# Six branch gates of a hybrid decoder layer computed by seven half-size products, spread between the branch products

## The chip, the cores and the metric

The kernel runs on one core of a Trainium2 chip. The metric is the device time of one execution in microseconds (us); lower is better. Engines are named as in the profile: PE is the matrix engine (TensorE), PEld its weight loads, DVE is VectorE, ACT is ScalarE, POOL is GpSimd, and SP issues most of the DMA transfers.

## The reference, cut to what matters

One decoder layer over 512 tokens of width 1024: a gated feed-forward half step, a mixer (dilated attention beside an mLSTM), and a second half step. The change is in the mixer's last part, the merge:

```python
A = dilated sliding-window attention        # att: (512, 512)
M = mLSTM matrix memory                     # ml:  (512, 1024)
merged = sigmoid(g_A) * (att @ W_A) + sigmoid(g_M) * (ml @ W_M)
x = x + RMSNorm_post(merged @ W_out)
# g_A, g_M: 1024 columns each of the input projection h @ W_in, h = RMSNorm_pre(x), (512, 1024)
```

Everything is float32.

## The kernel before

**How products are made.** PE multiplies in a reduced format (fp32r), so each operand is split into a high part (an ACT cast) and a low part (a DVE subtraction), and each product is three: high by high, high by low, low by high. The normalised activations lie transposed, 128 columns of the width by 512 tokens per block, as `hTh` and `hTl` (eight such blocks each). `load_w` loads a weight tile of 128 x 1024 (512 KB) into one of three `wf` buffers, casts it into one of five `wh` buffers (line 86) and subtracts into one of five `wl` buffers (line 88). `ws` (line 178) then issues, for a width of 8 blocks, 24 matmuls of 512 columns.

**Feed-forward parts.** Both already use a scheme of seven half-size products (Strassen's, in Winograd's form): a 2 x 2 block product is made from seven products of half size instead of eight, with sums of weight blocks and of activation blocks made first, and sums of the results afterwards. There a class `Order` (line 249) fixes the order on DVE, ACT and SP by hand.

**The merge.** The merged width has eight blocks, `dt` = 0 to 7. For each, `branch_gates(dt)` makes both gates, `wgm[dt, 0]` and `wgm[dt, 1]`, by two calls of `ws` (48 matmuls of 512 columns, row `p<-hTh_mx,wh_gm` in the profile), and ACT takes tanh of both into `t1` (line 1104). Gates 0 and 1 are made while the last mLSTM head is finished. The loop over `dt` then makes the two branch products, attention in 12 matmuls (`p2[0]`) and mLSTM in 24 (`p2[1]`), multiplies them with the gates (DVE, line 1150), adds (line 1151), splits the sum into `meTh` (ACT, line 1152) and `meTl` (DVE, line 1153), and ends with `branch_gates(dt + 2)`. After the loop, `down` multiplies by W_out in 192 matmuls (`acc_o`), and the results pass through the post norm into `xs`, the four tiles that hold x through the whole kernel.

**What sets the order.** Each engine runs its own instructions in one fixed order and waits at an instruction for what that needs. Outside the `Order` class that order is not the text's: a scheduler in the language's tile layer lays all instructions out with its own notion of their durations, and buffers (`bufs=5`) come free when their last reader is done.

Of the kernel before, what the change touches and what calls it, by code (L numbers as in the profile page):

```python
# [32 lines left out]
WMAX = 1024  # L33
# [6 lines left out]
def tile_hybrid_block(ctx: ExitStack, tc: tile.TileContext, a: dict):  # L40
    nc = tc.nc

    ids = ctx.enter_context(tc.tile_pool(name="ids", bufs=1))
    wpool = ctx.enter_context(tc.tile_pool(name="wpool", bufs=1))
    hpool = ctx.enter_context(tc.tile_pool(name="hpool", bufs=1))
    const = ctx.enter_context(tc.tile_pool(name="const", bufs=1, side="right"))
    act = ctx.enter_context(tc.tile_pool(name="act", bufs=1, side="right"))
# [10 lines left out]
    work = Work()  # L58
# [20 lines left out]
    def load_w(src, name, n=1024, after=()):  # L79
        wf = act.tile([P, WMAX], F32, tag="wf", bufs=3, name=f"wf_{name}")[:, :n]  # L80
        nc.sync.dma_start(wf, src)
        with ExitStack() as st:
            for i in after:
                st.enter_context(tc.issue_after(i))
            wh = wpool.tile([P, WMAX], F32R, tag="wh", bufs=5, name=f"wh_{name}")[:, :n]
            nc.scalar.copy(wh, wf)  # L86
            wl = wpool.tile([P, WMAX], F32R, tag="wl", bufs=5, name=f"wl_{name}")[:, :n]
            nc.vector.tensor_tensor(wl, wf, wh.bitcast(F32), op=ALU.subtract)  # L88
        return wh, wl

    def gain(src, name, eng=None):
        g = work.tile([P, D], F32, tag="gain", bufs=2, name=f"g_{name}")
        (eng or nc.gpsimd).dma_start(g, src.partition_broadcast(P))
        return g
# [16 lines left out]
        nc.vector.scalar_tensor_tensor(v, ss[:, 0:1], (4 if half else 1) * EPS, ss[:, 1:2], op0=ALU.add, op1=ALU.add)  # L111
        return rsqrt(v, 1, name)

    xs = [const.tile([P, D], F32, name=f"x{t}") for t in range(NT)]

    dram = ctx.enter_context(tc.tile_pool(name="dram", bufs=1, space=bass.MemoryType.DRAM))

    def scratch(name, *where):
# [55 lines left out]
    def ws(out, w, nk, xh, xl, tok=slice(0, T)):  # L174
        wh, wl = w
        terms = [(wh, x, k) for k in range(nk) for x in (xh, xl)] + [(wl, xh, k) for k in range(nk)]
        for n, (wt, x, k) in enumerate(terms):
            nc.tensor.matmul(out, lhsT=wt[:, k * P:(k + 1) * P], rhs=x[:, k, tok], start=n == 0,  # L178
                             stop=n == len(terms) - 1)
# [45 lines left out]
    def step(out, xh, xl, wh, wl, t, b, first, last):  # L225
        tk = slice(t * P, (t + 1) * P)
        cs = slice(b * 512, (b + 1) * 512)
        for n, (x, w) in enumerate(((xh, wh), (xl, wh), (xh, wl))):
            nc.tensor.matmul(out, lhsT=x[:, tk], rhs=w[:, cs], start=first and n == 0, stop=last and n == 2,  # L229
                             skip_group_check=True)  # L230
# [178 lines left out]
    class Down:  # L409
# [8 lines left out]
        def tt(self, out, p, q, op):  # L418
            self.do("vector", "tensor_tensor", out, p, q, op=op)
# [74 lines left out]
        def product(self, s):  # L494
            k, g = s[0], int(s[1])
            (xh, xl), (wh, wl) = self.x.pop(s), self.w.pop(s)
            if k in "pq":
                for b in range(2):
                    for i in range(2):
                        step(self.accs[i + 2 * (k == "q")][b], xh[:, i * P:], xl[:, i * P:], wh, wl, 0, b, False, False)  # L500
                return
            for n, (x, w) in enumerate(((xh, wh), (xh, wl), (xl, wh))):
                for m in range(2):
                    for i, o in enumerate(self.out[k]):
                        tk, cs = slice(m * H + i * P, m * H + (i + 1) * P), slice(m * T, (m + 1) * T)
                        nc.tensor.matmul(o, lhsT=x[:, tk], rhs=w[:, cs], start=k in "1256" and g + m + n == 0,
                                         stop=False, skip_group_check=True)
# [132 lines left out]
    with new_pool("ffn_a") as fa:  # L640
# [11 lines left out]
        for t in range(2):  # L652
            h = prenorm_first(t, g_pre, (hbuf + tbuf)[t])
# [6 lines left out]
        for t in range(2, NT):  # L660
            h = prenorm_first(t, g_pre, (hbuf + tbuf)[t], turned)
# [20 lines left out]
    hTh, hTl = hT  # L682
# [188 lines left out]
    def m_qk_proj(h, pi, between=None):  # L871
        pq = pair(f"pm{h}{pi}")
        w = [load_w(a["wmqk"][h, 2 * pi + b], f"mqk{h}{pi}{b}") for b in range(2)]
        ws(pq[0], w[0], KD, hTh, hTl)
        if between is not None:
            between()
        ws(pq[1], w[1], KD, hTh, hTl)
        return pq
# [15 lines left out]
        nc.vector.tensor_tensor(lo, zz, hi.bitcast(F32), op=ALU.subtract)  # L894


    pq0 = [pair(f"pq0{g}") for g in range(2)]
    w0 = [[load_w(a["wqk"][0, g, b], f"qk0{g}{b}", after=pins if g + b else ()) for b in range(2)] for g in range(2)]
    by_halves([(pq0[g], w0[g]) for g in range(2)], hTh, hTl, todo)
    for g in range(2):  # L900
        qk_of[0, g] = qk_evac(0, g, pq0[g])
    qk_proj(0, 2)
    for half in range(2):
        v0_proj(half)
    v12 = v12_proj(0)
# [188 lines left out]

    t1s = {}

    def branch_gates(dt):
# [4 lines left out]
        t1 = work.tile([P, 2, T], F32, tag=("h", "tmp")[dt % 2], bufs=1, name=f"t1_{dt}")  # L1102
        for b in range(2):
            nc.scalar.activation(t1[:, b, :], p1[b], AF.Tanh, scale=0.5)
        t1s[dt] = t1

    E = m_decay(0)
    for h in range(MH):
        vm, so = m_vo(h)
        EE = m_scores(h, qk, E)  # L1110
        if h + 1 < MH:
            qk = new_mqk(h + 1)
            m_qk_conv(h + 1, 0, m_qk_proj(h + 1, 0), qk)
        else:
            branch_gates(0)
        m_out(h, EE, vm, so)
        if h + 1 < MH:
            m_qk_conv(h + 1, 1, m_qk_proj(h + 1, 1), qk)
            E = m_decay(h + 1)
        else:  # L1120
            branch_gates(1)
        m_turn(h, so)
    lctx.close()

# [2 lines left out]
    mg = gctx.enter_context(tc.tile_pool(name="merge", bufs=1))  # L1127
# [8 lines left out]
            return mlT[k // 2][self.i][:, k % 2, tok]  # L1136

    mlTh, mlTl = Tiles(0), Tiles(1)
    wA = None
    for dt in range(KD):  # L1140
        if dt % 2 == 0:
            wA = load_w(a["wA"][dt // 2], f"wA{dt}")
        wM = load_w(a["wM"][dt], f"wM{dt}")
        p2 = pair(f"p2_{dt}")
        o = (dt % 2) * 512
        ws(p2[0], (wA[0][:, o:o + 512], wA[1][:, o:o + 512]), HEADS, atth, attl)
        ws(p2[1], wM, KD, mlTh, mlTl)
        t1 = t1s[dt]
        for b in range(2):
            nc.vector.scalar_tensor_tensor(t1[:, b, :], t1[:, b, :], 1.0, p2[b], op0=ALU.add, op1=ALU.mult)  # L1150
        nc.vector.tensor_tensor(t1[:, 0, :], t1[:, 0, :], t1[:, 1, :], op=ALU.add)
        nc.scalar.mul(meTh[:, dt, :], t1[:, 0, :], 0.5)
        nc.vector.scalar_tensor_tensor(meTl[:, dt, :], t1[:, 0, :], 0.5, meTh[:, dt, :].bitcast(F32),
                                       op0=ALU.mult, op1=ALU.subtract)
        if dt + 2 < KD:
            branch_gates(dt + 2)

    g_mpost = gain(a["mix_post_g"], "mpost")
    g_f2pre = gain(a["ffn2_pre_g"], "f2pre")
    hT2 = []  # L1160
# [117 lines left out]
```

## Time and profile before

| | |
|---|---|
| median of 3 runs | 1358.43 us (1358.39 to 1358.49) |
| profiled execution | 1358.6 us, span of its instructions 1356.8 us |
| PE busy | 1342.3 us of the span |
| DVE / ACT busy | 967.8 / 601.7 us |
| merge loop, first branch product to first W_out product | about 131 us, from 831.4 to 961.9 us |
| W_out product and post norm after it | from 961.9 us on |
| granted PE clock, mean | 0.998 |

A row of a group reads: source line, engine, operation, output <- inputs, shape, count | busy us in all, mean ns of one | idle time of that engine just before, and what ended it. A row of the timeline begins with start and length in us.

### The profile page before, as it was taken

To read this page: it belongs to the slowest core of one execution; us is meant where nothing else is said; L and a number is where in the kernel's file an instruction comes from. 1 tells how busy PE (TensorE), PEld (TensorE's weight loads), DVE (VectorE), ACT (ScalarE), POOL (GpSimd) and SP (SyncE) were. 2 spreads that over 40 slices of the span, in tenths; PEclk is the share of its full clock that TensorE was granted. 3 is DMA by queue.
4 is the path that set the end of the run, shared out by engine and by line. 5 is a ranking of instruction groups with operands and counts; after the bars stand their busy time and mean duration, and the time that the engine had idled before them with its cause. 6 is when DMAs were issued, how large, how long until landed. Compare 5 with 4: busy or idle time off the path is not lost.

```text
span 1356.8 us, 19908 instructions
## 1 busy us (share of the span) xinstructions
PE 1342.3 (99%) x7976; PEld 1192.8 (88%) x7976; DVE 967.8 (71%) x1482; ACT 601.7 (44%) x969; POOL 32.8 (2%) x56
## 2 busy tenths in 40 slices
PE   8999999999999999999999999999999999999998
PEld 8899999878898888888888888888889999998786
DVE  7799898996772885775756754334378798997983
ACT  5444444554633532445535443222264444444552
POOL 1000000000200000000000000000010000000000
PEclk9999999999999999999999999999999999999999
DMA  5233333654233422422222232233213333335541
GB/s 202 93 109 103 106 104 109 232 174 152 66 95 118 140 82 89 144 74 78 78 78 78 79 117 73 102 97 109 93 46 111 94 97 107 108 106 196 173 148 62
DMA packets 41661, 150.11 MB, mean 111 GB/s; under 512 B 4716, under 2 KB 4716, under 8 KB 41312
## 3 DMA queue, kind: packets, MB, share of 16 engines
q1 hardware_dynamic: 39600, 141.08, 31.7%
q0 software_dynamic: 1968, 7.76, 1.8%
q8 instruction: 62, 1.02, 0.3%
q14 instruction: 31, 0.25, 0.1%
HBM read 144.63 MB, written 4.19 MB: 110 GB/s over the span
## 4 chain that ended last, share of the span: by engine, by line
PE 89%; DVE 6%; ACT 2%; issue 2%; DMA 1%; SPq 0%; DVEq 0%; POOLq 0%; ACTq 0%
PE p L178 11%; PE qb_b L321 9%; PE qb_a L321 9%; PE pq L178 8%; PE pm L178 6%; PE qa_a L321 4%; PE qa_b L321 4%; PE acc_o L229 3%; PE pvo L997 2%; PE pvo L999 2%; PE pvo L998 2%; PE pg_a L188 2%; PE pg_b L188 2%; PE pq L188 2%; PE pg_b L178 2%; PE pg_a L178 2%
## 5 line engine op out<-in xcount | busy, mean ns | idle before, releaser
L178 PE MATMUL pq<-hTh_mx,wh_qk 128*128 128x512 f32 x160 | 63.2, 395 | 0.0
L178 PE MATMUL pq<-hTl_mx,wh_qk 128*128 128x512 f32 x160 | 62.4, 390 | 0.0
L88 DVE TENSOR_TENSOR wl_qk<-wf_qk,wh_qk 128x1024 fp32r<-128x1024 f32 x24 | 29.3, 1220 | 40.2 <-ACT wh_qk L86 29.9
L178 PE MATMUL pm<-hTh_mx,wh_mqk 128*128 128x512 f32 x128 | 50.3, 393 | 0.0
L997 PE MATMUL pvo<-wh_vo,hTh_mx 128*128 128x512 f32 x128 | 50.2, 392 | 0.0
L178 PE MATMUL pm<-hTl_mx,wh_mqk 128*128 128x512 f32 x128 | 49.9, 390 | 0.0
L178 PE MATMUL p<-hTh_mx,wh_gm 128*128 128x512 f32 x128 | 49.9, 390 | 0.0
L999 PE MATMUL pvo<-wl_vo,hTh_mx 128*128 128x512 f32 x128 | 49.8, 389 | 0.0
L178 PE MATMUL p<-hTl_mx,wh_gm 128*128 128x512 f32 x128 | 49.8, 389 | 0.0
L998 PE MATMUL pvo<-wh_vo,hTl_mx 128*128 128x512 f32 x128 | 49.8, 389 | 0.0
L86 ACT CAST wh_qk<-wf_qk 128x1024 fp32r<-128x1024 f32 x24 | 25.0, 1045 | 54.1 <-PE pw L741 27.3
L1150 DVE SCALAR_TENSOR_TENSOR t<-t,p 128x512 f32<-128x512 f32 x16 | 11.0, 688 | 42.7 <-PE p L178 42.7
L88 DVE TENSOR_TENSOR wl_mqk<-wf_mqk,wh_mqk 128x1024 fp32r<-128x1024 f32 x16 | 19.6, 1222 | 29.7 <-ACT wh_mqk L86 25.3
L178 PE MATMUL pq<-hTh_mx,wl_qk 128*128 128x512 f32 x160 | 39.6, 389 | 0.0
L888 DVE SCALAR_TENSOR_TENSOR z<-pm,cw,z 128x511 f32<-128x511 f32 (+2 forms) x48 | 35.2, 742 | 1.4 <-ACT z L886 0.9
L249 ACT CAST wh_a<-cd_a 128x1024 fp32r<-128x1024 f32 x18 | 18.9, 1049 | 39.0 <-DVE cd_a L249 39.0
L321 PE MATMUL qa_a<-hTl_f,wh_a 128*128 128x256 f32 x144 | 36.1, 283 | 0.0
L321 PE MATMUL qa_b<-hTl_f,wh_b 128*128 128x256 f32 x144 | 36.1, 283 | 0.0
L321 PE MATMUL qa_a<-hTh_f,wh_a 128*128 128x256 f32 x144 | 36.1, 283 | 0.0
L321 PE MATMUL qa_b<-hTh_f,wh_b 128*128 128x256 f32 x144 | 36.1, 283 | 0.0
L249 ACT CAST wh_b<-cd_b 128x1024 fp32r<-128x1024 f32 x18 | 18.9, 1049 | 37.9 <-DVE cd_b L249 37.9
L178 PEld LDWEIGHTS pq<-hTh_mx,wl_qk 128*128 128x128 f32 x160 | 30.0, 188 | 6.2
(679 smaller groups left out, 4396.3 us busy)
## 6 DMA issues: line engine op xcount, KB each, us to landing
wf_qk<-in_wqk SPq DMA_DIRECT2D x24, 512.0 KB, 3.6
B_a<-in_wdq SPq DMA_DIRECT2D x21, 512.0 KB, 3.8
B_b<-in_wdq SPq DMA_DIRECT2D x21, 512.0 KB, 4.4
g_a<-in_wgu SPq DMA_DIRECT2D x18, 512.0 KB, 3.7
u_a<-in_wgu SPq DMA_DIRECT2D x18, 512.0 KB, 3.8
g_b<-in_wgu SPq DMA_DIRECT2D x18, 512.0 KB, 3.8
u_b<-in_wgu SPq DMA_DIRECT2D x18, 512.0 KB, 3.8
wf_mqk<-in_wmqk SPq DMA_DIRECT2D x16, 512.0 KB, 3.3
```

The source lines that it names most:

```text
L86: nc.scalar.copy(wh, wf)
L88: nc.vector.tensor_tensor(wl, wf, wh.bitcast(F32), op=ALU.subtract)
L178: nc.tensor.matmul(out, lhsT=wt[:, k * P:(k + 1) * P], rhs=x[:, k, tok], start=n == 0, stop=n == len(terms) - 1)
L188: nc.tensor.matmul(outs[b][:, tok], lhsT=ws_[b][w][:, k * P:(k + 1) * P], rhs=x[:, k, tok], start=i + k + hf == 0, stop=hf == 1 and i == 2 ...
L229: nc.tensor.matmul(out, lhsT=x[:, tk], rhs=w[:, cs], start=first and n == 0, stop=last and n == 2, skip_group_check=True)
L249: self.last[eng] = getattr(getattr(nc, eng), fn)(*args, **kw).ins
L321: nc.tensor.matmul(out, lhsT=wt[:, i * P:(i + 1) * P], rhs=y[:, i, :], start=first and n == 0, stop=last and n == len(terms) - 1, skip_gro ...
L888: nc.vector.scalar_tensor_tensor(z[:, s:], src[:, :T - s], cw[:, ct, 3 - s:4 - s], z[:, s:], op0=ALU.mult, op1=ALU.add)
L997: nc.tensor.matmul(out, lhsT=hTh[:, k, tk], rhs=wh[:, cs], start=k == 0, stop=False)
L998: nc.tensor.matmul(out, lhsT=hTl[:, k, tk], rhs=wh[:, cs], start=False, stop=False)
L999: nc.tensor.matmul(out, lhsT=hTh[:, k, tk], rhs=wl[:, cs], start=False, stop=k == KD - 1)
L1150: nc.vector.scalar_tensor_tensor(t1[:, b, :], t1[:, b, :], 1.0, p2[b], op0=ALU.add, op1=ALU.mult)
```

## The change

Gates 2 to 7 are made by seven products of half size. Gates 0 and 1 stay as they were.

- `make_parts` builds, beside the end of mLSTM head 3, the sums of activation blocks: four full blocks (`full`), four differences, and their splits `part5`, `part7`, `part4`; the block that `hTh`/`hTl` hold in one corner is overwritten by part 6 once gate 1 is made. Parts 5 and 7 lie in the tiles of x, part 4 in the tiles of the gains.
- To free those, x is stored to DRAM (`xkeep`) before the mixer and loaded back into `xs` after the merge loop, by POOL's DMA queue; the gains `g_mpost` and `g_f2pre` are loaded after it, once part 4 has been read.
- `unit` makes one gate pair: it loads both weight tiles as `g` and `u`, makes four sums of half tiles (DVE), casts and subtracts 3.5 tiles' worth of weights in four takes (`(1,2)`, `(4)`, `(7,5)`, `(6,3)`), and issues 7 x 12 matmuls of 256 columns into two PSUM banks, `qa` (products 1, 2) and `qb` (6, 7 and 4 in one half, 5 and 3 in the other). Product 2 is added in the bank to product 1, after ACT has copied product 1 out (`q1`). DVE adds the rest in four steps.
- `unit` is a generator with three stops, and the loop takes it up between the branch products: products 1, 6, 5 after `p2[0]`, products 2, 7, 3 after `p2[1]`, product 4 after the next block's `p2[0]`.

```diff
+    def unit(n, srcs, r, q1, first_out):
+        g, u = (act.tile([P, 2, Q], F32, tag="wf", bufs=3, name=f"{'gu'[b]}_{n}") for b in range(2))
+        for t, src in zip((g, u), srcs):
+            nc.sync.dma_start(t, src.rearrange("p (q c) -> p q c", c=Q))
...
+        take((1, 2), g)
+        take((4,), u[:, 1:2, :])
+        tt(u[:, 1, :], u[:, 0, :], u[:, 1, :], ADD)
+        tt(u[:, 0, :], g[:, 0, :], u[:, 0, :], SUB)
+        tt(g[:, 0, :], u[:, 1, :], g[:, 0, :], SUB)
+        tt(g[:, 1, :], g[:, 1, :], g[:, 0, :], SUB)
+        take((7, 5), u)
+        take((6, 3), g)
+        pa, pb = bank(f"qa_{n}"), bank(f"qb_{n}")
+        qa, qb, qc = pa[:, 0:H], pb[:, 0:H], pb[:, H:T]
...
+        product(qa, 1, True, False)
+        nc.scalar.copy(q1, qa)
+        product(qb, 6, True, False)
+        product(qc, 5, False, False)
+        tt(r[:, :, H:T], pb.rearrange("p (a b) -> p a b", b=H), q1[:, None, :].broadcast_to([P, 2, H]), ADD)
+        yield
+        product(qa, 2, False, True)
+        first_out(r[:, 0, 0:H], qa)
+        product(qb, 7, False, False)
+        tt(r[:, 1, H:T], qb, r[:, 1, H:T], ADD)
+        product(qc, 3, False, True)
+        tt(r[:, 0, H:T], qc, r[:, 0, H:T], ADD)
+        yield
+        product(qb, 4, False, True)
+        tt(r[:, 1, 0:H], qb, q1, ADD)
+        yield
...
+    for t in range(NT):
+        nc.gpsimd.dma_start(xkeep[t], xs[t])
...
         ws(p2[0], (wA[0][:, o:o + 512], wA[1][:, o:o + 512]), HEADS, atth, attl)
+        for _ in late_gates:
+            pass
+        next(gates_, None)
         ws(p2[1], wM, KD, mlTh, mlTl)
+        next(gates_, None)
...
-        if dt + 2 < KD:
-            branch_gates(dt + 2)
-
+        late_gates = gates_
+
+    xs[:] = new_xs()
+    for t in range(NT):
+        nc.gpsimd.dma_start(xs[t], xkeep[t])
```

The order that the scheduler makes of it is shown at three places of block `dt` = 4. First PE. Before, the block's 36 branch matmuls (`p2_4_0`, `p2_4_1`) and then the 48 of gate 6 (`p1_6`) follow each other, each group on a PSUM bank of its own:

```order
L178 MATMUL p2_4_0_8316<-atth_3891,wl_wA4_8308 128x512 x4
L178 MATMUL p2_4_1_8317<-mlm0h0_6539,wh_wM4_8312 128x512
...
L178 MATMUL p2_4_1_8317<-mlEh3_7816,wl_wM4_8314 128x512 x2
L178 MATMUL p1_6_0_8371<-hTh_mx_3745,wh_gm60_8361 128x512
...
L178 MATMUL p1_6_1_8372<-hTh_mx_3745,wl_gm61_8369 128x512 x8
L178 MATMUL p2_5_0_8430<-atth_3891,wh_wA4_8306 128x512
```

Now, behind `p2_4_0` stand products 7, 3 and 4 of gate 5 (`wh7`, `wh6`, `wh4`; a tile holds two products' weights and has the first one's number), product 1 of gate 6 around product 4, then product 2 of gate 6 (`wh1` again) and product 6 (`wh6`):

```order
L180 MATMUL p2_4_0_8550<-atth_3891,wl_wA4_8542 128x512 x4
L959 MATMUL qb_gm5_8431<-part7h_7632,wh7_gm5_8422 128x256
...
L959 MATMUL qb_gm5_8431<-hTh_mx_3745,wh6_gm5_8426 128x256
...
L959 MATMUL qa_gm6_8604<-hTh_mx_3745,wh1_gm6_8584 128x256
L959 MATMUL qb_gm5_8431<-part4h_7638,wh4_gm5_8414 128x256
...
L959 MATMUL qa_gm6_8604<-hTh_mx_3745,wl1_gm6_8585 128x256 x4
L959 MATMUL qa_gm6_8604<-hTh_mx_3745,wh1_gm6_8584 128x256
...
L959 MATMUL qb_gm6_8605<-hTh_mx_3745,wh6_gm6_8600 128x256
```

Product 2, which the text has behind `p2[1]`, was moved up to stand directly behind product 1 in the same half bank, and the scheduler took products 7, 3 and 4 of a gate out from among the branch matmuls into one run.

Second DVE, from the multiplication of block 3's mLSTM product on. Before:

```order
L1150 SCALAR_TENSOR_TENSOR t1_3_8067<-t1_3_8067,p2_3_1_8197 128x512
L88 TENSOR_TENSOR wl_gm60_8363<-wf_gm60_8359,wh_gm60_8361 128x1024
L1151 TENSOR_TENSOR t1_3_8067<-t1_3_8067 128x512
L1153 SCALAR_TENSOR_TENSOR meTl_7835<-t1_3_8067,meTh_7834 128x512
L88 TENSOR_TENSOR wl_gm61_8369<-wf_gm61_8365,wh_gm61_8367 128x1024
```

Now (line 943 are the sums of weights and of results, 243 the subtractions of `take`):

```order
L1261 SCALAR_TENSOR_TENSOR t1_3_8062<-t1_3_8062,p2_3_1_8377 128x512
L88 TENSOR_TENSOR wl_wM4_8548<-wf_wM4_8544,wh_wM4_8546 128x1024
L1262 TENSOR_TENSOR t1_3_8062<-t1_3_8062 128x512
L1261 SCALAR_TENSOR_TENSOR t1_4_8236<-t1_4_8236,p2_4_0_8550 128x512
L1264 SCALAR_TENSOR_TENSOR meTl_7867<-t1_3_8062,meTh_7866 128x512
L943 TENSOR_TENSOR t1_5_8404<-qb_gm5_8431,q1_gm5_8405 128x2x256
L943 TENSOR_TENSOR t1_5_8404<-qb_gm5_8431,t1_5_8404 128x256
L243 TENSOR_TENSOR wl1_gm6_8585<-g_gm6_8580,wh1_gm6_8584 128x1024
```

The sixth row empties products 6 and 5 of gate 5 from `qb`, which product 7 in the PE rows above needs; five instructions of block 3 and 4 stand ahead of it.

Third ACT in the same block. Before, five casts and two steps of gate 4 and block 3:

```order
L86 CAST wh_wA4_8306<-wf_wA4_8304 128x1024
L1104 ACTIVATE t1_4_8187<-p1_4_1_8138 128x512
L86 CAST wh_wM4_8312<-wf_wM4_8310 128x1024
L86 CAST wh_gm60_8361<-wf_gm60_8359 128x1024
L1152 ACTIVATE meTh_7834<-t1_3_8067 128x512
L86 CAST wh_gm61_8367<-wf_gm61_8365 128x1024
```

Now:

```order
L1263 ACTIVATE meTh_7866<-t1_3_8062 128x512
L1189 ACTIVATE t1_5_8404<-qa_gm5_8430 128x256
L242 CAST wh1_gm6_8584<-g_gm6_8580 128x1024
L242 CAST wh4_gm6_8588<-u_gm6_8581 128x512
L242 CAST wh7_gm6_8596<-u_gm6_8581 128x1024
L1191 ACTIVATE t1_5_8404<-t1_5_8404 128x768
L963 COPY q1_gm6_8579<-qa_gm6_8604 128x256
L242 CAST wh6_gm6_8600<-g_gm6_8580 128x1024
```

The copy of product 1 (`q1_gm6`) stands behind the cast of gate 6's weight sums (`wh7`) and the long tanh of gate 5, and the cast `wh6` behind the copy. In this block `wh6` takes the buffer of `wh1` of the same gate, so it also waits for product 2.

More of the change, by code (lines that the diff above doesn't have):

```diff
@@ L112, in mean_rsqrt, with new_xs @@
         return rsqrt(v, 1, name)
-    xs = [const.tile([P, D], F32, name=f"x{t}") for t in range(NT)]
+    def new_xs():
+        return [const.tile([P, D], F32, tag=f"x{t}", bufs=1, name=f"x{t}") for t in range(NT)]
+    xs = new_xs()
     dram = ctx.enter_context(tc.tile_pool(name="dram", bufs=1, space=bass.MemoryType.DRAM))
@@ L894, in m_qk_conv, with make_parts, quad, part @@
         nc.vector.tensor_tensor(lo, zz, hi.bitcast(F32), op=ALU.subtract)
+    x7 = {}
+    def make_parts(t, take):
+        def quad(t, i, j):
+            return t[:, 4 * i:4 * i + 4, j * H:(j + 1) * H]
+        x7.update({k: (quad(hTh, i, j), quad(hTl, i, j)) for k, (i, j) in {1: (0, 0), 2: (1, 0), 3: (1, 1)}.items()})
+        full = lambda out, i, j: nc.vector.tensor_tensor(out, quad(hTh, i, j).bitcast(F32), quad(hTl, i, j).bitcast(F32),
+                                                         op=ADD)
+        sub_ = lambda out, p, q: nc.vector.tensor_tensor(out, p, q, op=SUB)
+        def part(k, src, h, l):
+            split(src, h, l)
+            x7[k] = (h, l)
+        full(t[0], 0, 1)
+        full(t[1], 0, 0)
+        sub_(t[1], t[0], t[1])
+        part(5, t[1], *take(5))
+        full(t[2], 1, 1)
+        sub_(t[1], t[2], t[1])
+        sub_(t[0], t[2], t[0])
+        part(7, t[0], *take(7))
+        full(t[3], 1, 0)
+        sub_(t[3], t[3], t[1])
+        part(4, t[3], *take(4))
+        yield
+        part(6, t[1], quad(hTh, 0, 1), quad(hTl, 0, 1))
+        yield
@@ new lines, in unit, with take, product @@
+    def unit(n, srcs, r, q1, first_out):
+        g, u = (act.tile([P, 2, Q], F32, tag="wf", bufs=3, name=f"{'gu'[b]}_{n}") for b in range(2))
+        for t, src in zip((g, u), srcs):
+            nc.sync.dma_start(t, src.rearrange("p (q c) -> p q c", c=Q))
+        w = {}
+        def take(keys, src):
+            m = len(keys)
+            wh, wl = (wpool.tile([P, WMAX], F32R, tag=f"w{y}", bufs=5, name=f"w{y}{keys[0]}_{n}")[:, :m * Q]
+                      .rearrange("p (q c) -> p q c", c=Q) for y in "hl")
+            split(src, wh, wl)
+            for i, k in enumerate(keys):
+                w[k] = (wh[:, i, :], wl[:, i, :])
+        tt = lambda out, p, q, op: nc.vector.tensor_tensor(out, p, q, op=op)
+        take((1, 2), g)
[8 more added lines that the diff above has]
+        qa, qb, qc = pa[:, 0:H], pb[:, 0:H], pb[:, H:T]
+        def product(out, k, first, last):
+            (wh, wl), (xh, xl) = w[k], x7[k]
+            terms = [(wh, y, i) for i in range(4) for y in (xh, xl)] + [(wl, xh, i) for i in range(4)]
+            for m, (wt, y, i) in enumerate(terms):
+                nc.tensor.matmul(out, lhsT=wt[:, i * P:(i + 1) * P], rhs=y[:, i, :], start=first and m == 0,
+                                 stop=last and m == len(terms) - 1, skip_group_check=True)
+        product(qa, 1, True, False)
[10 more added lines that the diff above has]
+        tt(r[:, 0, H:T], qc, r[:, 0, H:T], ADD)
+        yield
+        product(qb, 4, False, True)
+        tt(r[:, 1, 0:H], qb, q1, ADD)
+        yield
@@ L897, in tile_hybrid_block @@
+    xkeep = [dram.tile([P, D], F32, name=f"xkeep{t}") for t in range(NT)]
     pq0 = [pair(f"pq0{g}") for g in range(2)]
@@ L1095, in tile_hybrid_block, with branch_gates @@
     t1s = {}
-    def branch_gates(dt):
+    def branch_gates(dt, seven=True):
+        t1 = t1s[dt] = work.tile([P, 2, T], F32, tag=("h", "tmp")[dt % 2], bufs=1, name=f"t1_{dt}")
+        if seven:
+            q1 = mg.tile([P, H], F32, tag="q1", bufs=2, name=f"q1_gm{dt}")
+            yield from unit(f"gm{dt}", [a["wgm"][dt, b] for b in range(2)], t1, q1,
+                            lambda out, pa: nc.scalar.activation(out, pa, AF.Tanh, scale=0.5))
+            rest = t1.rearrange("p a b -> p (a b)")[:, H:]
+            nc.scalar.activation(rest, rest, AF.Tanh, scale=0.5)
+            yield
+            return
         wg = [load_w(a["wgm"][dt, b], f"gm{dt}{b}") for b in range(2)]
@@ L1101, in branch_gates, with take_part @@
             ws(p1[b], wg[b], KD, hTh, hTl)
-        t1 = work.tile([P, 2, T], F32, tag=("h", "tmp")[dt % 2], bufs=1, name=f"t1_{dt}")
         for b in range(2):
             nc.scalar.activation(t1[:, b, :], p1[b], AF.Tanh, scale=0.5)
-        t1s[dt] = t1
+        yield
+    def take_part(k):
+        if k == 4:
+            return [work.tile([P, D], F32R, tag="gain", bufs=2, name=f"part4{y}").rearrange("p (a b) -> p a b", b=H)
+                    for y in "hl"]
+        return [const.tile([P, 4, H], F32R, tag=f"x{k // 7 * 2 + i}", bufs=1, name=f"part{k}{y}")
+                for i, y in enumerate("hl")]
     E = m_decay(0)
@@ L1114, in tile_hybrid_block @@
         else:
-            branch_gates(0)
+            room = [lp.tile([P, 8, H], F32, tag=f"mqk{x}", bufs=1, name=f"room{x}") for x in "hl"]
+            parts = make_parts([t[:, 4 * i:4 * i + 4, :] for t in room for i in range(2)], take_part)
+            next(parts)
+            next(branch_gates(0, False))
         m_out(h, EE, vm, so)
@@ L1120, in tile_hybrid_block @@
         else:
-            branch_gates(1)
+            next(branch_gates(1, False))
+            next(parts)
         m_turn(h, so)
@@ L1138, in tile_hybrid_block @@
     mlTh, mlTl = Tiles(0), Tiles(1)
-    wA = None
+    wA, late_gates = None, iter(())
     for dt in range(KD):
+        gates_ = branch_gates(dt + 2) if dt + 2 < KD else iter(())
         if dt % 2 == 0:
```

## The prediction, made before the changed kernel was run

> **What bounds the kernel now.** I read the page's busy times first, then the chain that ended last, then the merge as a window, then who waits in it.
>
> ```profile
> PE 1342.3 (99%) x7976; PEld 1192.8 (88%) x7976; DVE 967.8 (71%) x1482; ACT 601.7 (44%) x969; POOL 32.8 (2%) x56
> ...
> 66.15 2.88 PE qb_a L321 x24
> 70.47 4.32 PE qb_a L321 x36
> 76.23 2.88 PE qb_a L321 x24
> ...
> 831.43 130.59 PE p L178 x576
> 962.02 38.09 PE acc_o L229 x168
> ...
> 831.40:962.00 130.60, 130.60 (x578) 108.16 (x577) 48.25 (x55) 37.70 (x45) 0.00 (x0) 1.00 0.30 97
> ...
> DVE t L1150 <- PE p L178: 42.7, 16, 4.8
> ACT meTh L1152 <- DVE t L1151: 22.7, 7, 3.3
> ```
>
> The merge is one piece of the chain, 576 matmuls without a gap: 130.59 / 576 = 0.227 us for 512 columns. DVE is busy 48.25 us of 130.60 and waits 42.7 us for PE; PE waits for nobody. The feed-forward part already runs seven-product units: rows 66.15 and 76.23 are one unit apart, 10.08 us for 84 matmuls, 0.120 us for 256 columns. So PE is the bound, and what counts is PE work saved less any wait that PE gets.
>
> **The PE work.** A plain gate pair is 48 x 0.227 = 10.90 us, a unit 84 x 0.120 = 10.08. Six pairs save 6 x 0.82 = 4.9 us. (The Trainium skill, "TensorE: Matmul & The Clock Gate", section Back-to-back issue gap, gives N / 2.4 + 2.5 ns for warm matmuls, 109 and 216 ns; by it a pair would save 1.2 us and six 7 us. The rows are slower at both sizes, and the measurement decides.)
>
> **What PE now waits for.** Products of one gate share two PSUM banks, and DVE and ACT empty them step by step. I take the order shown for block 4 and walk it with durations of these rows:
>
> ```profile
> L88 DVE TENSOR_TENSOR wl_gm<-wf_gm,wh_gm 128x1024 fp32r<-128x1024 f32 x16 | 19.6, 1224 | 20.7 <-PE p L178 12.5 <-ACT wh_gm L86 8.2
> L1150 DVE SCALAR_TENSOR_TENSOR t<-t,p 128x512 f32<-128x512 f32 x16 | 11.0, 688 | 42.7 <-PE p L178 42.7
> L249 DVE TENSOR_TENSOR z_a<-qb_a,uv_a 128x256 f32<-128x256 f32 x36 | 13.6, 419 | 1.1 <-PE qb_a L321 0.3
> L86 ACT CAST wh_gm<-wf_gm 128x1024 fp32r<-128x1024 f32 x16 | 16.8, 1048 | 41.2 <-PE p L178 29.7 <-PE pvo L998 8.9 <-PE pm L178 2.6
> L1152 ACT ACTIVATE meTh<-t 128x512 fp32r<-128x512 f32 x8 | 5.1, 632 | 22.7 <-DVE t L1151 22.7
> L249 ACT COPY q_a<-qa_a 128x256 f32<-128x256 f32 x18 | 6.7, 373 | 9.9 <-PE qa_a L321 9.9
> ...
> 839.66 0.69 DVE L1150 SCALAR_TENSOR_TENSOR t<-t,p 128x512 f32<-128x512 f32 x1 [4.75 <-PE p L178]
> 840.27 1.22 DVE L88 TENSOR_TENSOR wl_gm<-wf_gm,wh_gm 128x1024 fp32r<-128x1024 f32 x1
> 841.40 0.68 DVE L1151 TENSOR_TENSOR t<-t 128x512 f32<-128x512 f32 x1
> ...
> 71.59 0.69 DVE L249 TENSOR_TENSOR cd_a<-ab_a,u_a 128x512 f32<-128x512 f32 x1
> 72.31 0.69 DVE L249 TENSOR_TENSOR cd_a<-cd_a,g_a 128x512 f32<-128x512 f32 x1
> ...
> 66.47 1.04 ACT L249 CAST wh_a<-ab_a 128x1024 fp32r<-128x1024 f32 x1
> 67.40 1.05 ACT L249 CAST wh_a<-g_a 128x1024 fp32r<-128x1024 f32 x1
> ...
> 61.31 0.52 PE L321 MATMUL qa_a<-hTh_f,wl_a 128*128 128x256 f32 x3
> 61.67 0.28 PE L321 MATMUL qb_a<-x6h_a,wh_a 128*128 128x256 f32 x1
> 61.87 0.37 ACT L249 COPY q_a<-qa_a 128x256 f32<-128x256 f32 x1 [6.22 <-PE qa_a L321]
> ```
>
> On DVE 1024 columns take 1.22 us and the next starts after 1.13; 512 take 0.69 (0.61; 0.72 where the next needs the result); 256 take 0.42. On ACT 1024 take 1.05 (0.93). The last rows give the handover: product 1 ends at 61.83, 0.16 after the next product may start (61.67), and its copy starts 0.04 later; the copy ends at 62.24. In the feed-forward product 6 goes to another bank meanwhile. In the merge product 2 comes next, in the bank being copied.
>
> Block 4 (even), from its first attention matmul, in us. PE has issued the 12 by 2.73. DVE, free for block 3's end at 0.21, does its multiply, the subtraction for wM (0.82), the add (1.95, done 2.64), then the multiply of `p2_4_0` (2.93), `meTl` (3.55, after ACT's `meTh`), and the emptying of products 6 and 5 of gate 5 (4.29 to 4.98). Product 7 starts at 5.03: **wait 2.3**. It is issued by 6.47, its add ends 7.11, product 3 starts 7.16: **wait 0.7**. Five matmuls of product 1 follow, product 4 (wait 0.1), the rest of product 1, issued by 11.57. ACT is then in `wh7` (free from 11.39, when DVE has made the weight sums) and in a tanh of 768 columns (0.73 to the next by the lengths of the 512 and 1024 rows), so the copy runs 13.06 to 13.48 and product 2 starts 13.53: **wait 2.0**. The cast `wh6` must wait until product 2's high matmuls have left its buffer (14.70), ends 15.74, and product 6 starts 15.79: **wait 0.8**. The rest, 24 of 256 and 24 of 512 columns, needs 8.3 us and nothing it lacks. Sum 5.9 us; the block lasts 24.1.
>
> Block 5 (odd), same walk: product 1 of gate 7 follows the attention product and waits for its cast, whose buffer wA's last high matmul frees at 2.0 (0.4), then for its low part behind four DVE instructions (0.7); product 2 waits for the copy alone (0.7); product 3 for an add (0.1); product 4 for an add that stands behind two weight sums (0.7); product 6 for the last weight sum and `wh6` (1.0). Sum 3.6; it lasts 21.8.
>
> Block 0 holds the copy and the `wh6` wait (1.5), blocks 1, 3, 5 are odd, 2 and 4 even, 6 and 7 hold none: 1.5 + 3 x 3.6 + 2 x 5.9 = 24.1, taken as **24 us of waits**.
>
> Does PE really stand in such waits, and at what price? One place in the down product shows it:
>
> ```profile
> 1252.50 1.08 PE L506 MATMUL accc_b<-wh_b,xh_b 128*128 128x512 f32 x4
> 1253.27 0.61 ACT L249 CAST xh_b<-S_b 128x512 fp32r<-128x512 f32 x1
> 1253.93 0.50 PE L506 MATMUL accb_b<-wh_b,xh_b 128*128 128x512 f32 x1 [0.35 <-ACT xh_b L249]
> 1254.27 1.09 PE L506 MATMUL accc_b<-wl_b,xh_b 128*128 128x512 f32 x4
> ```
>
> The cast ends 1253.88, the matmul starts 0.05 later, and the next follows after 0.34 instead of 0.227: 0.11 more where new weights are loaded with nothing ahead. Twelve of the waits end in new weights, 1.3 us more at most; I take half, 0.6.
>
> **What I cost at nothing.** The parts are made while PE finishes head 3 and gate 1, the last 30 us before the merge:
>
> ```profile
> 801.00:831.40 30.40, 30.40 (x161) 26.30 (x160) 13.59 (x32) 12.43 (x24) 1.93 (x3) 1.00 0.26 87
> ```
>
> DVE is busy 13.59 us of 30.40 there. The parts add 12 instructions of 1024 columns, 12 x 1.13 = 13.6 us (ACT four casts, 4 us), and gate 2's weights three such and five of 512, 3 x 1.13 + 5 x 0.61 = 6.4: 33.6 in all, a little over the stretch, less two plain subtractions (2.3) that go with the plain gate 2. So DVE runs nearly through, and gate 2 comes last on it. In my walk PE meets this only behind product 1 of gate 2, in waits counted above; if a sum came later, the 31.3 - 30.4 us left over and one instruction more, 0 to 2 us: taken 0. Storing x: POOL issues it between its small powers in the post norm; an issue is over before the next power's input is there; 0 to 1. Loading x and the two gains:
>
> ```profile
> g_mpost<-in_mix_post_g POOLq DMA_DIRECT2D x1, 512.0 KB, 5.2
> g_f2pre<-in_ffn_pre_g POOLq DMA_DIRECT2D x1, 512.0 KB, 4.7
> wf_gm<-in_wgm SPq DMA_DIRECT2D x16, 512.0 KB, 3.3
> ```
>
> Behind the last reader, product 4 of gate 7, PE still has block 7 (36 x 0.227 = 8.2 us) and more than 100 W_out matmuls (23 us) before the first post norm needs a gain or x; six transfers one after the other at 5.2 take 31 us, and they may overlap. That just fits; were it one transfer short, it would cost up to 5 us. Weight loads on SP stay 512 KB each, as many as before, 3.3 us to landing in blocks of over 20 us.
>
> **The sum.** Against the profiled 1358.6 us (span 1356.8 and 1.8 around it; the median of the runs is 0.2 lower): -4.9 + 24.1 + 0.6 = +19.8, so 1378.4, and 1378.2 against the median. I say **1378**.
>
> **Rivals.**
> *PE stays fed, faster.* If products 1 to 7 found their banks and weights ready, 1358.4 - 4.9 = 1353.5. For it: DVE has 82 us of room in the merge and ACT 93. Against: room is not order; each wait above is one queue's place. It decides at 1.64 us of waits per two blocks; the walk has 9.4. Chance 3 in 100, with 2 more for waits that just cancel the saving (1356 to 1361).
> *Waits about half as long,* since ACT and DVE start some casts and sums earlier than my walk has it (a buffer freed sooner, handovers hidden): -4.9 + 12 gives 1365.5. Against it, the waits hang on instructions with measured lengths; chance 10.
> *The clock drops.* At the opening PE idles between short groups:
>
> ```profile
> 5.00:10.00 5.00, 2.83 (x19) 1.87 (x17) 2.02 (x5) 2.78 (x5) 1.11 (x2) 1.00 1.00 367
> 10.00:15.00 5.00, 4.15 (x23) 3.76 (x24) 5.00 (x8) 5.00 (x9) 0.00 (x0) 0.77 0.69 281
> 15.00:20.00 5.00, 5.00 (x41) 5.00 (x40) 4.56 (x8) 2.53 (x4) 2.04 (x2) 0.89 0.61 205
> ```
>
> After PE was busy 2.83 of 5 us the granted clock was 0.77 and 0.89 of full speed: 0.23 x 5 + 0.11 x 5 = 1.7 us lost. An even block has PE busy 1.4 in 3.7 us once; if each of the five blocks with waits lost that, 1378 + 8.5 = 1386.5. Against: the longest wait is 2.3 us, and matmuls stand around it, where the opening had mostly transposes. Chance 12. (The Trainium skill, same page, Part 1, has the clock halved after a fully idle window of about 3.4 us; by that rule no drop comes, and the time stays 1378. No row here settles it.)
>
> **How the numbers follow.** The forecast (1372 to 1383: hidden parts and handovers, 30 waits at up to 0.15 either way, 5 us) has 73 in 100. The range 1364 to 1385 takes in the half waits and part of the clock's case. Faster by over 0.2%, about what a measurement of this kernel can tell from no change: 3 in 100; within 0.2%: 2; slower: 95.
>
> **What would show it.** The PE group `qb_gm` has idle time before it, ended by DVE `t1` and ACT `wh`, and `qa_gm` by ACT `q1`; together some 24 us. The merge window lasts 149 to 151 us with PE busy about 126; granted clock 1.00 in it. The head of each even block shows one wait of over 2 us before product 7. The mLSTM part before and W_out after it keep their lengths. If PE's waits there sum to under 10 us, the walk is wrong; if the mLSTM or the post norm grew, a cover that I cost at nothing was gone.

## The result: 1382.2 us, 23.8 us slower, all of it in the merge

The changed kernel takes 1382.19 us (median of 4 runs, 1381.49 to 1382.52) against 1358.41; the ratio is 1.0175, interval 1.0163 to 1.0187. The profiled execution took 1381.49 us, the shortest of the four; its span is 1379.7, 22.9 more than before. (The other three had a mean granted clock of 0.993 to 0.994 where it had 0.996.) The busy times of the page after:

```profile
PE 1347.4 (98%) x8192; PEld 1201.9 (87%) x8192; DVE 1017.7 (74%) x1554; ACT 616.4 (45%) x991; POOL 37.1 (3%) x64
```

PE has 216 matmuls more (six gates of 84 small ones for 48 large ones) and DVE 50 us more work. The same three stretches as windows, the end of the mLSTM part, the merge, and the W_out product; each row begins with the window and its length, then come the busy times (and instructions) of PE, PEld, DVE, ACT and POOL, then the granted clock. First before, then after:

```profile
801.00:831.20 30.20, 30.20 (x161) 26.10 (x159) 13.39 (x32) 12.39 (x23) 1.93 (x3) 1.00 0.26 88
831.20:961.90 130.70, 130.70 (x580) 108.26 (x578) 48.45 (x55) 37.74 (x45) 0.00 (x0) 1.00 0.30 97
961.90:1000.10 38.20, 38.20 (x171) 31.61 (x170) 16.80 (x26) 11.89 (x25) 2.21 (x4) 1.00 0.22 69
```

```profile
801.00:831.00 30.00, 30.00 (x159) 25.91 (x158) 26.40 (x46) 13.77 (x26) 1.38 (x2) 1.00 0.11 36
831.00:984.70 153.70, 135.95 (x796) 117.49 (x795) 84.13 (x113) 49.33 (x65) 3.23 (x6) 0.98 0.31 106
984.70:1023.00 38.30, 38.30 (x172) 31.71 (x171) 17.44 (x27) 13.00 (x26) 2.22 (x4) 1.00 0.26 85
```

The merge grew from 130.7 to 153.7 us; the stretches around it kept their lengths, though DVE is now busy 26.4 of 30.0 us in the first. In the merge PE is no longer busy all the time, and the granted clock is 0.98. Whom PE waits for there (us in total, times, longest):

```profile
PE qb_gm L959 <- DVE t L943: 6.3, 7, 2.1
PE qa_gm L959 <- ACT q_gm L963: 4.9, 6, 1.7
PE qb_gm L959 <- ACT wh_gm L242: 4.5, 6, 0.8
PE qa_gm L959 <- DVE wl_gm L243: 1.4, 3, 0.5
PE qa_gm L959 <- ACT wh_gm L242: 0.7, 3, 0.2
```

These 25 waits sum to 17.8 us. Idle time is counted from the modelled end of the last matmul, and an unhindered matmul starts 0.16 before that (quoted in the prediction), so they cost 17.8 + 25 x 0.16 = 21.8 us. How one looks, the first of block 1, with the two matmuls behind it:

```profile
849.80 0.39 PE L959 MATMUL qa_gm<-hTh_mx,wh_gm 128*128 128x256 f32 x1 [0.23 <-ACT wh_gm L242]
850.02 0.28 PE L959 MATMUL qa_gm<-hTl_mx,wh_gm 128*128 128x256 f32 x1
850.14 0.29 PE L959 MATMUL qa_gm<-hTh_mx,wh_gm 128*128 128x256 f32 x1
```

The second follows after 0.22 us, the third after 0.12. The other waits at full clock show the same 0.10, so the restarts cost 25 x 0.10 = 2.5 us. Most of the rest is clock. It falls in block 4, after the wait for product 7: windows of 3.41 us, the granted clock is the third number from the end (1.00, 0.50, 0.50):

```profile
916.97:920.38 3.41, 1.30 (x7) 0.80 (x6) 2.75 (x5) 1.01 (x2) 0.00 (x0) 1.00 0.48 154
920.38:923.79 3.41, 2.89 (x14) 2.60 (x14) 0.93 (x2) 1.05 (x1) 0.00 (x0) 0.50 0.00 0
923.79:927.20 3.41, 3.41 (x18) 3.41 (x18) 1.52 (x3) 0.62 (x1) 0.00 (x0) 0.50 0.00 0
```

For 6.82 us PE ran at half speed; block 4 lasts 26.7 us where block 2, with the same order of PE and the full clock, lasts 24.4. That is 2.3 us more although its wait for the copy is 0.3 shorter (1.39 against 1.67), so the clock cost about 2.6.

DVE in that block shows who is late. These are all its instructions from the addition of block 3 to the emptying of products 6 and 5 of gate 5:

```profile
917.05 0.68 DVE L1262 TENSOR_TENSOR t<-t 128x512 f32<-128x512 f32 x1
918.03 0.69 DVE L1261 SCALAR_TENSOR_TENSOR t<-t,p 128x512 f32<-128x512 f32 x1 [0.29 <-PE p L180]
918.64 0.68 DVE L1264 SCALAR_TENSOR_TENSOR meTl<-t,meTh 128x512 fp32r<-128x512 f32 x1
919.36 0.69 DVE L943 TENSOR_TENSOR t<-qb_gm,q_gm 128x512 f32<-128x512 f32 x1
```

The emptying ends at 920.05 and product 7 starts at 920.10. It stands behind `meTl` of block 3 (918.64), and that is no accident of the scheduler: gate 5's result tile takes the buffer of gate 3's (`tag=("h", "tmp")[dt % 2]`, one buffer each), and `meTl` is the last to read gate 3's.

### The profile page after: what moved, and what is told of

It is laid out like the page before. It is cut to its first block, busy times and chain, and to the rows that moved or that the text cites. A ratio compares the mean times of both kernels' runs of the same rounds, so it can differ in the third digit from the quotient of the medians.

```text
span 1379.7 us, 20470 instructions
## 1 busy us (share of the span) xinstructions
PE 1347.4 (98%) x8192; PEld 1201.9 (87%) x8192; DVE 1017.7 (74%) x1554; ACT 616.4 (45%) x991; POOL 37.1 (3%) x64
## 5 line engine op out<-in xcount | busy, mean ns | idle before, releaser
L180 PEld LDWEIGHTS pq<-hTh_mx,wh_qk 128*128 128x128 f32 x160 | 30.1, 188 | 6.0
L180 PEld LDWEIGHTS pq<-hTl_mx,wh_qk 128*128 128x128 f32 x160 | 30.1, 188 | 6.0
```

## Experiments

Theory A: the 24 us are places in the queues, made by buffers and order, and the same work in another place would leave PE fed. Theory B: DVE and ACT have too much to do for each block. "The walk" is the walk of the prediction, made for each kernel's own fixed order.

**Without the units.** Gates 2 to 7 plain again, all else kept.

```diff
-        gates_ = branch_gates(dt + 2) if dt + 2 < KD else iter(())
+        gates_ = iter(())
...
+        if dt + 2 < KD:
+            next(branch_gates(dt + 2, False))
```

> The changed kernel with gates 2 to 7 made by the plain 48 matmuls again; x still goes to DRAM and back, the gains are still loaded late, and the sums of activation blocks are still made but not used (the plain gates then read one corner of hTh and hTl that part 6 has overwritten). What I cost at nothing is nothing: 1358.4 us, merge window 130.6 to 130.9 us. Rival, some of the 23.8 us come from the parts on DVE or from x and the gains arriving late in the post norm: 1360 to 1366 us, with PE idle before the merge or behind the W_out product.

Measured 1358.23 us, ratio 1.0002 (0.9993 to 1.0012). What the prediction cost at nothing costs nothing here (gate 2's own weight sums are not in this run):

```profile
801.00:831.30 30.30, 30.30 (x161) 26.17 (x160) 25.12 (x43) 15.88 (x27) 5.48 (x8) 1.00 0.48 174
831.30:961.90 130.60, 130.60 (x578) 108.15 (x577) 49.48 (x56) 37.77 (x46) 0.00 (x0) 1.00 0.28 97
```

DVE does 12 us more before the merge and PE never waits.

**A third result tile.**

```diff
-        t1 = t1s[dt] = work.tile([P, 2, T], F32, tag=("h", "tmp")[dt % 2], bufs=1, name=f"t1_{dt}")
+        t1 = t1s[dt] = (mg if dt % 3 == 2 else work).tile([P, 2, T], F32, tag=("h", "tmp", "t1x")[dt % 3], bufs=1, name=f"t1_{dt}")
...
```

> The changed kernel with three result tiles for the gates instead of two (the third in the space of the last two blocks of the merged activations). In the changed kernel the result tile of gate dt+2 is that of gate dt, so the sum that empties products 6 and 5 must wait for the last steps of block dt. Theory A (places in the queues, the buffer of the result first): the waits of product 7, product 4 and wA go; walking the fixed order of this kernel leaves 12.6 us of waits, nearly all on the copy of product 1 (0.7, 1.6 and 2.4 us a block) and the cast for product 6, and the merge takes 138.5 us plus 1 to 3 us of restarts and clock: 1369 to 1373 us. Theory B (DVE and ACT have too much to do for each block): the same work stands on the same engines, 1380 to 1383 us.

Measured 1365.73 us (ratio 1.0055, 1.004 to 1.007), 16.5 us less than the changed kernel. All waits of PE left in the merge:

```profile
PE qa_gm L959 <- ACT q_gm L963: 7.5, 6, 1.4
PE qb_gm L959 <- ACT wh_gm L242: 2.1, 3, 0.7
```

The waits on `t`, `wl_gm` and wA are gone, as theory A has it, and the copy's grew from 4.9 to 7.5. The merge took 138.0 us (walk 138.5) at full clock. The time lies below the 1369 to 1373 us that I expected: that range does not follow from its own sum, since 1358.4 + 138.5 - 130.7 is 1366.2, and 1 to 3 us on top make 1367 to 1369.

The buffer was not the only thing to change. With a tile free the scheduler laid out another order. On PE product 7 now stands behind the mLSTM product, ahead of the next attention product, and on DVE the emptying of products 6 and 5 (first row, block 3) stands ahead of that block's multiplication of the mLSTM product, no longer behind `meTl`:

```profile
901.85 0.69 DVE L943 TENSOR_TENSOR t<-qb_gm,q_gm 128x512 f32<-128x512 f32 x1 [2.42 <-PE qb_gm L959]
906.86 0.69 DVE L1270 SCALAR_TENSOR_TENSOR t<-t,p 128x512 f32<-128x512 f32 x1 [4.31 <-PE p L180]
```

So the 16.5 us are the tile and the order that it allowed, together with the clock that was no longer lost. The work stayed the same, so theory B is out for two thirds of the loss.

**The copy earlier as well.** The casts of the weight sums move behind the copy in the text.

```diff
-        take((7, 5), u)
-        take((6, 3), g)
...
         nc.scalar.copy(q1, qa)
+        take((6, 3), g)
+        take((7, 5), u)
```

> The third result tile again, and in the text of a gate the casts of the weight sums (products 6, 3 and 7, 5) moved behind the copy of product 1; the scheduler still sets every order. Theory A: ACT no longer stands in a cast of weight sums when product 1 ends, so the waits on the copy fall from 8.5 us (seen with the third tile alone) to about 3, and the walk leaves 7.4 us of waits, merge 133.3 us: 1360.8 us, up to 1363 with restarts. Theory B (the work on ACT and DVE): the casts only move, 1364 to 1366 us as with the third tile alone.

Measured 1361.61 us (1.0027, 1.0016 to 1.0038):

```profile
PE qb_gm L957 <- ACT wh_gm L242: 2.6, 3, 1.1
PE qa_gm L957 <- ACT q_gm L961: 1.9, 3, 0.7
PE qa_gm L957 <- ACT wh_gm L242: 0.4, 2, 0.2
```

The copy's waits fell from 7.5 to 1.9 us. They had come mostly from ACT's queue. With the third tile alone the copy stood behind a cast of weight sums and a long tanh (first three rows); now the casts stand behind it (last three), and what is left is the tanh:

```profile
895.18 1.05 ACT L242 CAST wh_gm<-u_gm 128x1024 fp32r<-128x1024 f32 x1 [3.53 <-DVE u_gm L943]
896.13 0.84 ACT L1191 ACTIVATE t<-t 128x768 f32<-128x768 f32 x1
896.87 0.35 ACT L963 COPY q_gm<-qa_gm 128x256 f32<-128x256 f32 x1
...
912.87 0.85 ACT L1191 ACTIVATE t<-t 128x768 f32<-128x768 f32 x1 [3.85 <-DVE t L943]
913.62 0.35 ACT L961 COPY q_gm<-qa_gm 128x256 f32<-128x256 f32 x1
914.19 1.05 ACT L242 CAST wh_gm<-g_gm 128x1024 fp32r<-128x1024 f32 x1 [0.22 <-DVE g_gm L943]
```

Here too the scheduler changed PE's order as well, so the share of ACT's queue alone is not shown.

**Three banks for each gate.**

```diff
-        qa, qb, qc = pa[:, 0:H], pb[:, 0:H], pb[:, H:T]
+        qa, qb, qc = (bank(f"q{x}_{n}")[:, 0:H] for x in "abc")
...
```

> The changed kernel with products 5 and 3 in a PSUM bank of their own (three banks for each gate, the two emptying sums apart). Theory A: only waits of product 3 and 4 on the emptying of the shared bank can go, and the walk gives the time back at product 6 in odd blocks (2.2 us instead of 1.0): merge 147.6 us without restarts, 2.2 less than the changed kernel, so 1379 to 1381 us. Rival C (the shared banks make the waits): more than 10 us gone, under 1372 us.

Measured 1378.94 us (1.0153, 1.0138 to 1.0168): 3.2 us less than the changed kernel, so rival C falls. The wait for the cast before product 6 rose from 4.5 to 9.2 us:

```profile
PE qb_gm L958 <- ACT wh_gm L242: 9.2, 6, 2.1
```

What one wait gave up, the next one took: 20 waits sum to 18.0 us of idle time where the changed kernel has 25 with 17.8. The little that was gained is mostly fewer restarts and less time at half clock, 3.41 us against 6.82 in the profiled executions.

**The order of the text on PE.**

```diff
+    do = Order()
...
-                nc.tensor.matmul(out, lhsT=wt[:, i * P:(i + 1) * P], rhs=y[:, i, :], start=first and m == 0,
+                do("tensor", "matmul", out, lhsT=wt[:, i * P:(i + 1) * P], rhs=y[:, i, :], start=first and m == 0,
...
+        wA = load_w(a["wA"][dt // 2][:, (dt % 2) * 512:(dt % 2) * 512 + 512], f"wA{dt}", 512)
...
```

Both branch products are issued through the same `do`.

> The changed kernel with the order of the text pinned on PE alone: products 1, 6, 5 behind the attention product, 2, 7, 3 behind the mLSTM product, 4 behind the next attention product; DVE, ACT and the buffers of the results as the scheduler has them (the weights of the attention product are loaded in halves, so that five buffers suffice for this order). Rival D (product 2 directly behind product 1 makes the waits, spreading the products as the text has it cures them): the copy is hidden by products 6 and 5, 6 to 10 us less than the changed kernel, 1372 to 1376 us. Theory A (the result tile of gate dt+2 is that of gate dt, so in any order of PE the emptying of products 6 and 5 waits for the last steps of block dt): product 7 then waits 3.4 us in every block, 29.6 us of waits in all, merge 155.6 us, slower than the changed kernel: 1385 to 1394 us with restarts and some time at half clock.

Measured 1402.06 us (1.0319, 1.0305 to 1.0333), slower still by 20 us. Spreading the products, which the text asks for, is worse while the result tile is shared:

```profile
PE qb_gm L252 <- DVE t L946: 22.8, 12, 3.3
831.90:1005.90 174.00, 149.09 (x794) 131.46 (x793) 85.97 (x117) 51.16 (x69) 3.24 (x6) 0.86 0.31 100
```

Product 7 waits 3.3 us in each of six blocks, as theory A said. The merge is 174.0 us, not 155.6 and a few: each of those waits cost clock as well (0.86 over the merge), 47.8 us at half speed in all, far more than I allowed. Of the 20 us about 6 are longer waits (24.9 us idle in 18 of them, each 0.16 more); most of the rest is clock.

**The order by hand.** PE, DVE, ACT and the weight loads run in the order in which this kernel's own text has them, in each block this one (the casts and sums of the next gate's weights stand between):

```python
plain(p2[0], [t[:, o:o + 512] for t in roles["A"]], HEADS, atth, attl)
...
product(prev.qb, f"4{prev.dt % 2}", 0, 4, False, True)     # product 4 of the gate before
...
product(u.qa, "1", 0, 1, True, False)
do("scalar", "copy", u.q1, u.qa)
plain(p2[1], roles["M"], KD, mlTh, mlTl)
finish()                                                   # block dt's last steps
u.result()                                                 # only now gate dt+2's result tile
product(u.qb, "6", 0, 6, True, False)
product(u.qc, "7", 1, 5, True, False)
...
product(u.qa, "1", 1, 2, False, True)
...
product(u.qb, "7", 0, 7, False, False)
...
product(u.qc, "6", 1, 3, False, True)
```

> The same products and sums, two result tiles, but the order of PE, DVE, ACT and of the weight loads in the merge is written by hand: attention product, product 4 of the gate before, product 1, mLSTM product with block dt's last steps, products 6, 5, 2, 7, 3; weights are cast and summed about a block ahead into buffers with fixed roles; products 5 and 3 have a bank of their own, the weights of product 4 a small tile of their own. Theory A: the walk finds no wait at all in the merge, 125.9 us; 1358.4 - 4.9 = 1353.5 us, up to 1355 with restarts. Theory B (too much work on DVE and ACT in each block): waits of 10 us or more stay in any order, over 1363 us.

> The order by hand once more, with two small tiles for the weights of product 4, one for odd and one for even gates (with one tile, the kernel before had made product 4 with the weights of the next gate). The work and its order on each engine stay: the walk finds no wait in the merge. Theory A: 1353.5 us, between 1353 and 1355. If the one tile had hidden a wait for product 4: up to 1356.

The first has one small tile for the weights of product 4, so it makes that product with the next gate's weights; the second, whose code is shown, has two. The first took 1353.62 us (0.9966, 0.9955 to 0.9978), the second 1353.87 (0.9966, 0.9952 to 0.9979): 4.1 us faster than before, 28.3 faster than the changed kernel. No wait of PE is left in the merge of the second:

```profile
PE 1336.8 (99%) x8192; PEld 1198.4 (89%) x8192; DVE 1017.2 (75%) x1560; ACT 616.2 (46%) x991; POOL 37.2 (3%) x64
830.90:957.20 126.30, 126.30 (x795) 114.67 (x794) 86.98 (x123) 50.08 (x66) 3.24 (x6) 1.00 0.39 134
```

DVE does 87.0 us of work in 126.3, more than the 84.1 that it did in 153.7 of the changed kernel. Theory B is out: the same products and sums, with more DVE work than the changed kernel, leave PE fed. Two result tiles suffice here, because block `dt` is finished before gate `dt + 2` needs its tile.

**The order by hand with the shared bank.**

```diff
-            self.qa, self.qb, self.qc = (bank(f"q{x}_gm{self.dt}")[:, 0:H] for x in "abc")
+            pa, pb = bank(f"qa_gm{self.dt}"), bank(f"qb_gm{self.dt}")
+            self.qa, self.qb, self.qc = pa[:, 0:H], pb[:, 0:H], pb[:, H:T]
...
-            product(u.qc, "7", 1, 5, True, False)
+            product(u.qc, "7", 1, 5, False, False)
```

> The order by hand, with products 5 and 3 in the other half of the bank of products 6, 7 and 4, as the changed kernel has them. Theory A says that the places in the order make the waits, and the shared bank is one such: product 3 stands directly behind product 7 and may not start until the sum on DVE that reads product 7 from the same bank is done, 1.0 us in each block and 2.1 in the first, 7.0 us by the walk: 1360.5 us. If reading one half of a bank does not hold up writing the other: 1353.5 to 1354.5 us.

Measured 1360.30 us (1.0017, 1.0008 to 1.0027), 6.4 us more than with three banks and already slower than the kernel before:

```profile
PE qb_gm L251 <- DVE t L251: 4.2, 6, 0.8
```

Six waits, one a block, for product 3 (the shared bank has one name, `qb_gm`). None is as long as the 2.1 us that I had walked for the first. The program makes PE wait for a read of the other half; whether the chip would need that was not tried.

**What costs clock.**

```diff
+    IDLE = (1, 5, 4, 7, 3, 9)
...
+        if u and IDLE[dt]:
+            d = bank(f"idle{dt}")[:, 0:H]
+            do("tensor", "matmul", d, lhsT=x7[1][0][:, 0, 0:P], rhs=x7[1][0][:, 0, :], start=True, stop=True)
+            do("scalar", "copy", z, d)
+            for _ in range(IDLE[dt] - 1):
+                do("scalar", "copy", z, z.bitcast(F32))
+            do("tensor", "matmul", d, lhsT=z[:, 0:P], rhs=x7[1][0][:, 0, :], start=True, stop=True)
```

> The order by hand, with a stop of PE of chosen length at the end of blocks 0 to 5: a small matmul waits for 1, 5, 4, 7, 3 and 9 copies in a row on ACT, so PE stands about 1.4, 2.4, 1.9, 3.3, 1.5 and 5.4 us; else PE is fed. It asks which stops cost clock. Theory E (a stop costs clock from some length on, and that is over 3 us): the granted clock falls after the stops of blocks 3 and 5 only. Theory F (2 us can be enough, by where the stop falls): it falls after one or both of blocks 1 and 2 too. By the walk 1372 us without clock loss, up to 1390 us if each long stop costs 3 us. The Trainium skill, TensorE: Matmul & The Clock Gate, Part 1, has the clock fall after a whole idle window of about 3.4 us; by it theory E.

Measured 1377.60 us (1.014, 1.0122 to 1.0159). The stops came out at 0.5, 2.2, 1.8, 3.1, 1.3 and 7.8 us without a matmul; the last is longer than meant because ACT stood 2.94 us in the middle of the copies, before a cast whose W_out tile had not landed. The clock fell after the 3.1 and in the 7.8, not at the others. Windows around the 2.2, the 3.1 and the 7.8:

```profile
865.35:868.76 3.41, 2.29 (x20) 2.09 (x18) 3.31 (x6) 2.24 (x5) 0.00 (x0) 1.00 0.06 22
868.76:872.17 3.41, 2.32 (x11) 1.93 (x12) 3.23 (x4) 1.92 (x4) 0.00 (x0) 1.00 0.11 23
...
909.72:913.13 3.41, 0.83 (x4) 0.74 (x5) 2.60 (x4) 3.25 (x7) 0.00 (x0) 1.00 0.00 0
913.13:916.54 3.41, 3.41 (x10) 2.62 (x9) 1.23 (x1) 0.07 (x1) 0.00 (x0) 0.50 0.79 231
916.54:919.95 3.41, 3.41 (x28) 3.29 (x28) 1.11 (x2) 0.93 (x2) 0.00 (x0) 1.00 0.19 77
...
954.09:957.50 3.41, 0.00 (x0) 0.00 (x0) 0.46 (x2) 1.25 (x4) 0.00 (x0) 1.00 1.03 390
957.50:960.91 3.41, 0.26 (x1) 0.26 (x2) 1.23 (x1) 2.16 (x4) 0.00 (x0) 0.50 0.41 168
```

Taken alone this run would bear out theory E. The changed kernel, whose 2.1 us cost clock, speaks against it.

**The changed kernel once more.**

> The changed kernel once more, for a second profile. Its first profile shows half clock after the wait of block 4 (2.1 us without a matmul) and none after the same wait of block 2. If the clock falls by where the wait lies in time, another execution shows it after other waits of about this length, or after both; if something of block 4 itself does it, it falls there again and only there. 1381 to 1383 us.

Measured 1381.91 us in a single execution. The half clock is in block 4 again, 6.82 us long, but 10 us later, behind the wait on the copy; block 2, and the wait for product 7 of block 4, kept the full clock:

```profile
916.51:919.92 3.41, 1.59 (x7) 0.97 (x6) 3.08 (x5) 1.01 (x2) 0.00 (x0) 1.00 0.47 143
926.75:930.16 3.41, 1.69 (x14) 1.48 (x14) 2.64 (x4) 2.06 (x4) 0.00 (x0) 1.00 0.00 0
930.16:933.57 3.41, 2.90 (x14) 2.51 (x13) 1.22 (x1) 1.01 (x1) 0.00 (x0) 0.50 0.55 167
```

So it is where the wait lies in time that decides, theory F: waits of the same length, at the same place of the program, cost clock in one execution and not in the other.

## The prediction, point by point

**PE work saved, 4.9 us: nearly right.** With PE fed throughout, the merge takes 126.3 us instead of 130.7, 4.4 less.

**24.1 us of waits: right in place, a little too large in sum.** The trace gives 21.8, by 25 waits, and five of 0.1 us that I had also counted do not show as idle time. The other 1.8 lie mostly in waits that came out up to 0.2 shorter than walked, and in block 4, where the half clock hid part of one. The long one before product 7 measured 2.1 + 0.16 against 2.3, and falls in blocks 2 and 4 only.

**The mechanism: right, one layer short.** I named the queue place of each wait ("each wait above is one queue's place") and took the place as the scheduler's choice. For the emptying of products 6 and 5 a buffer forbade an earlier one: with a third tile the scheduler moved it ahead, and 16.5 us came back with the order that followed. The sixth row of the DVE order shown with the change could have been read so, since it writes `t1_5` while the rows ahead still use `t1_3`.

**Handovers, 0.6 us: too small.** I charged half of 0.11 us to 12 waits that end in new weights. The trace has about 0.10 after every one of the 24 waits at full clock, whether PE had waited for weights or for something else: 2.5 us with the 25th.

**The clock: the rival came true in part, and the forecast left it out.** I gave 12 in 100 to five blocks that lose 1.7 us each. It was one block, and about 2.6 us. Its condition was misjudged: I argued that matmuls around a 2.3 us wait keep the clock, and once they did not.

Summed as measured: 1358.6 - 4.4 + 21.8 + 2.5 + 2.6 = 1381.1, and the five short waits, if they are there unseen, make it 1381.6; the profiled execution took 1381.5. The sum of the prediction, 1378.4, was about 3 us low against that. It left out the clock (2.6), had the restarts 1.9 too small and the saving 0.5 too large; it also had the waits 1.8 too large, and that this error took back part of the others is luck. The median is another 0.7 us longer, with the lower clock of the other three executions.

**What would show it.** Expected was a merge of 149 to 151 us with PE busy 126 at clock 1.00; it is 153.7, 136.0 and 0.98. PE's busy time holds the modelled ends (25 x 0.16 = 4.0 us), the restarts (2.5), the clock (2.6) and the five short waits (0.5): with the 126.3 of the order by hand that is 135.9.

**What I cost at nothing: right.** The parts, x through DRAM and the late gains cost 0 within 0.1%.

**The rivals.** "PE stays fed" failed for the reason given, that room is not order: DVE was busy 84 of 153.7 us while PE waited for it. In another order it came true, at 1353.9 (worked out: 1353.5). "Half the waits" failed; outside the stretch at half clock none that the trace shows was shorter than walked by more than about 0.2 us.

## What to carry to other kernels

When a unit of work is delayed to overlap the next one, ask first how long each of its results and its buffers is now held, and which later step gets the same buffer: here a third result tile, with the order that the scheduler then made, gave back 16.5 us, and an order by hand needed only two. With the tile shared, the order of the text was worse than the scheduler's by 20 us; whether a third tile would mend that order was not tried. A wait that is taken away alone is handed to the next one in the chain (three banks: the cast's wait doubled, and the waits together stayed as long), so walk the whole block in its new order before you count a gain. An engine with 45% spare time, as DVE in this merge, can still starve the one that is the bound.

## What the hardware showed that I had not expected

In the run with the chosen stops every change of the granted clock lies on one grid of 3.41 us: 913.13, 916.54, then 957.50, which is 13 steps of 3.413 after the first. The clock halves at the end of a window in which PE did little, not at a length of wait: PE was busy 0.83 and 0.00 of 3.41 us there, and 1.30 in the changed kernel. The stop of 2.2 us fell across two windows (2.29 and 2.32 us busy) and cost no clock. In the second execution of the changed kernel a window with 1.59 us busy (7 matmuls of 512 columns) kept the clock and one with 1.69 (14 of 256) lost it, so the limit lies about there and is not quite the busy time of this view. The Trainium skill, "TensorE: Matmul & The Clock Gate", Part 1, has windows of about 3.4 us, which these traces bear out, and has the clock fall after a whole idle one, which they do not: 1.30 of 3.41 us busy was idle enough. So in each execution of the changed kernel one wait of about 2 us brought 6.82 us at half clock, 2.6 us of time in the first. How a window is weighed was not settled.
